# Layer norm statistics by bn_stats on transposed tiles, and twelve weight tiles whose low part is made by ScalarE and an adding DMA

## The chip, the core and the metric

The program runs on one core of a Trainium2 chip. The metric is the device time of one execution in microseconds (us). Five engines take part: PE (TensorE, matmuls and transposes), DVE (VectorE), ACT (ScalarE), POOL (GpSimd) and SP (SyncE, which issues the transfers). Each engine works through its own instructions in the order in which they were written.

## What is computed

One step of a backbone of four layers over 640 tokens (128 context tokens, 512 latent tokens) with 1024 features. The mixers are differential attention (layer 0 and again layer 3), retention (layer 1) and a short gated convolution (layer 2). What matters here is the end of each layer, the normalization, and the start of the next:

```
def layer_norm(x, g, b):
    xf = x.astype(jnp.float32)
    mu = jnp.mean(xf, -1, keepdims=True)
    var = jnp.mean(jnp.square(xf - mu), -1, keepdims=True)
    return ((xf - mu) * lax.rsqrt(var + LN_EPS)).astype(x.dtype) * g + b
...
hs = xs * (1 + sc_s) + sh_s            # modulated input of a layer's projection
...
xs = layer_norm(ALPHA * xs + g_s * out_s, ln_g[i], ln_b[i])
```

`out_s` is the mixer's output times its output projection. The next layer's projection needs the normalized and modulated row, so it cannot start on a token before that token's mean and variance are known.

## The kernel before

**Layout.** The running x lies in SBUF feature-major: `xT[128, 8, 640]`, eight blocks m of 128 features, all tokens along the free axis. Every large product is made of three fp32r matmuls from a high and a low part of each operand: `hH`, `hL` for the modulated input, `yh`, `yl` for the mixer's output, and `wh`, `wl` for a weight tile. A weight tile arrives by DMA in `raw`; ACT copies it to `wh` (rounded to fp32r), and DVE (at times POOL) writes `wl = raw - wh` (`convert`). Four tiles of layers 1 to 3 do not go through the ring of `wh`/`wl` but into spare space (`RA`, `FB`). In the text "y,W matmuls" are those of the output projection, "h,W matmuls" those of the next layer's projection.

**A layer's end.** The tokens are worked in two halves, hf0 and hf1 (256 and 384 tokens; in layer 3 384 and 256). The output projection's last group runs over the eight m of hf0 and then the eight m of hf1; each result is added to `xT` by one or two DVE instructions (`xT<-ps,mod,xT`). Then class `LN` normalizes that half.

**Layer norm before.** Ahead of the last group an estimate of the mean is taken off x (`center`, `spread`, `sub_c`). As the m of a half arrive, ACT squares them (`FA<-xT`), and DVE or POOL add up x and the squares over m (`reduce`, rows `FA<-FA,xT` and `FA<-FA`). When both sums are there, PE sums over the 128 partitions with one-column matmuls against `onesm` (`sums`), which puts one token on a partition; DVE makes the variance and the inverse root by Newton steps on two or three columns (`rsqrt`), spreads it over a diagonal (`FA<-ident,sm`), and PE broadcasts it to all partitions (`bcast`, `FA,pick`). The mean goes a shorter way (`shift`, ACT copies it to `FA`), and `sub_mean` takes it off x from SBUF (`xT<-xT,FA`, on DVE or POOL). `normal` multiplies by the broadcast root from PSUM (`xT<-xT,ps`). Per m there follow the affine step twice (ACT writes `hH`, ACT or DVE the same in full precision into `FA`, row `FA<-xT,Av,Bv`) and `hL = FA - hH`. Then the h,W matmuls of that m may run.

**Order.** No order is written by hand. `plan` keeps streams of items (the mixer's, the layer norm's, the weights', the modulation vectors' `mods_all`, whose matmuls are the rows `mraw,cpad`) and takes, at each step, the item that a small model of the engines (`Clock`, with `LAT` for the delay from one engine to another) expects to start soonest. An item marked `now` is taken as soon as it can be. `xtt` and `affine` choose between two engines by the same model; `BIAS_T` is what the affine step's ACT version may be later than DVE's and still be taken. So a change of one item's engines shifts the order near it.

Of the kernel before, what the change touches and what calls it, by code (L numbers as in the profile page):

```python
# [13 lines left out]
I32 = mybir.dt.int32  # L14
# [33 lines left out]
BIAS_T = 0.0  # L48
# [16 lines left out]
N_W = 0  # L65
C_OP = 0
# [13 lines left out]
GATE_L = 2000.0  # L80
GATE_H = [4000.0, 4000.0]
# [3 lines left out]
class W:  # L85


    def __init__(self, src, n=1024, direct=False, own=None, after=()):
        self.src, self.n, self.direct = src, n, direct
        self.own, self.after = own, after  # L90
        self.raw = self.hi = self.lo = self.slot = None
        self.uses = 0
# [19 lines left out]
class Clock:  # L112
# [4 lines left out]
    ENG = ("PE", "ACT", "DVE", "POOL", "DMA")  # L117
    LAT = {
        "PE": (0.0, 280.0, 250.0, 250.0, 2000.0),
        "ACT": (197.0, 34.0, 128.0, 80.0, 2000.0),  # L120
        "DVE": (196.0, 145.0, 127.0, 74.0, 2000.0),
        "POOL": (197.0, 170.0, 155.0, 102.0, 2000.0),
        "DMA": (1400.0, 1400.0, 1400.0, 1400.0, 2000.0),
# [19 lines left out]
    def arr(self, d, name, n):  # L143
        a = d.get(name)
        if a is None or a.shape[1] < n:
            b = np.full((5, max(n, 400)), -1e4)
# [15 lines left out]
    def run(self, ops, commit, gate=4000.0, slack=250.0):  # L162
# [9 lines left out]
        for eng, dur, outs, ins, port in ops:  # L172
# [11 lines left out]
            for oi, oo, e, end in own:  # L184
                if e == row == 4:
                    continue
# [38 lines left out]
def kernel(ctx: ExitStack, tc: tile.TileContext, io: dict):  # L225
# [21 lines left out]
    onesm = sb("onesm", [128, 128])  # L247
# [21 lines left out]
    onesr = sb("onesr", [128, 1], F32R)  # L269
# [150 lines left out]

    def copymax(out, a, mx):
# [10 lines left out]
    def dma(out, in_):  # L432
# [5 lines left out]
        do("DMA", n * 4 / 360.0, [out] if sb_o else [], [in_] if sb_i else [], lambda: nc.sync.dma_start(out=out, in_=in_))  # L438

# [168 lines left out]
    def outproj_items(l, wname, gi, groups, final=False, ln=None, need=()):  # L608
# [37 lines left out]
        for i, (mp, mi, hf) in enumerate(order):  # L646
# [10 lines left out]
            if final:  # L657
                late = [("y", base + grp[-1], h) for h in range(2)] + [("c", l, hf, 2 * mp + mi) if l == 1 else ("c", l, 1, 7)]
# [9 lines left out]
    class LN:  # L668

        def __init__(self, l, hf):
            self.l, self.hf = l, hf
            self.c0, self.n = HALF_F[l][hf]
            n = self.n
            o = NF - 7 * T if hf == 0 else NF - 7 * n
            v = [FA[:, o + i * n:o + i * n + n] for i in range(7)]
            self.dg = v[0]
            o = 0 if hf == 0 else T - n
            self.sc = KD[:, o:o + n] if l == 1 else RA[:, 4096 + o:4096 + o + n]  # L680
            self.db = v[1]
            buf = {0: FA[:, 4864:], 1: None, 2: F2[:, 6432:], 3: FA[:, 4864:]}[l]
            self.cs = None if buf is None else buf[:, o:o + n]
            self.sd, self.q = v[2:4]
            self.sq = self.t = v[4:7]
# [4 lines left out]
        def center(self):  # L690
            xtt(self.sc, self.x(0), self.x(1), ALU.add, BIAS_L)

        def spread(self):
            ps = pj((self, 0))[:, 0:self.n]
            mm(ps, onesr.to_broadcast([128, 128]), self.sc, True, True)

            if self.cs is not None:
                act(self.cs, ps)
                done((self, 0))

        def sub_c(self, m):
            x = self.x(m)
            if self.cs is not None:
                xtt(x, x, self.cs, ALU.subtract, BIAS_C)
                return
            vtt(x, x, bank((self, 0))[:, 0:self.n], ALU.subtract)
            if m == 7:
                done((self, 0))

        def add_q(self, m):  # L710
            if m:
                xtt(self.q, self.q, self.sq[m % 3], ALU.add, BIAS_L)

        def reduce(self, m):
            x = self.x(m)
            act(self.sq[m % 3] if m else self.q, x, ACTF.Square)
            if m:
                xtt(self.sd, self.x(0) if m == 1 else self.sd, x, ALU.add, BIAS_L)
                self.add_q(m - 1)
            if m == 7:  # L720
                self.add_q(7)

        def sums(self, which, src):
            ps = bank((self, 1)) if which else pj((self, 1))
            for i in range(self.n // 128):
                o = 8 * which + 2 * i
                mm(ps[:, o:o + 1], src[:, 128 * i:128 * i + 128], onesm[:, 0:1], True, True)

        def shift(self):
            ps = pj((self, 0))[:, 0:self.n]  # L730
# [3 lines left out]
            done((self, 0))  # L734
# [69 lines left out]
        def items(self):  # L804
            l, hf = self.l, self.hf
            it = []
            for m in range(8):
                it.append(Item(lambda m=m: self.reduce(m), need=[("x", l, hf, m)]))
            it.append(Item(self.mean))
            it.append(Item(self.var))  # L810
            it.append(Item(self.shift, give=[("db", l, hf)]))
            it.append(Item(self.bcast, give=[("rb", l, hf)]))
            ap, lo, sm_ = [], [], []
            for m in range(8):
                sm_.append(Item(lambda m=m: self.sub_mean(m), need=[("db", l, hf)], give=[("ctr", l, hf, m)]))
                nd = [("rb", l, hf), ("ctr", l, hf, m)]
                if l + 1 < DEPTH:
                    ap.append(Item(lambda m=m: self.apply_t(m), need=nd + [("aff", l + 1)] + ([("lnh", l, hf, m - 3)] if m > 2 else []),
                                   give=[("t", l, hf, m)]))
                    lo.append(Item(lambda m=m: self.apply_lo(m), need=[("t", l, hf, m)], give=[("lnh", l, hf, m)]))  # L820
                else:
                    ap.append(Item(lambda m=m: self.output(m), need=nd))
            return it, ap, lo, sm_

        def c_items(self, need):
# [1014 lines left out]
```

## Time and profile before

| | us |
|---|---|
| runs | 1867.8, 1868.26, 1870.71 |
| median of the runs | 1868.26 |
| the profiled execution, its own time | 1870.52 |
| its span from first to last instruction | 1868.6 |
| mean granted TensorE clock in it | 0.974 of full speed |
| PE busy | 1785.9 (96%) |
| DVE busy | 1200.9 (64%) |
| ACT busy | 731.2 (39%) |
| POOL busy | 195.8 (10%) |

The times are those of whole executions; the span is what the trace covers, 1.9 us less. Busy shares are averages over the span. Between the layers they look otherwise: the stretch of a layer boundary runs here from the first y,W matmul of the last group to the h,W matmul with which the next layer's first groups of weight tiles are through on both halves. There are three, at about 433 to 506, 1057 to 1141 and 1383 to 1465 us, and a tail from 1822 us in which layer 3 is normalized and written out.

### The profile page before, as it was taken

To read this page: it belongs to the slowest core of one execution; us is meant where nothing else is said; L and a number is where in the kernel's file an instruction comes from. 1 tells how busy PE (TensorE), PEld (TensorE's weight loads), DVE (VectorE), ACT (ScalarE), POOL (GpSimd) and SP (SyncE) were. 2 spreads that over 40 slices of the span, in tenths; PEclk is the share of its full clock that TensorE was granted. 3 is DMA by queue.
4 is the path that set the end of the run, shared out by engine and by line. 5 is a ranking of instruction groups with operands and counts; after the bars stand their busy time and mean duration, and the time that the engine had idled before them with its cause. 6 is when DMAs were issued, how large, how long until landed. Compare 5 with 4: busy or idle time off the path is not lost.

```text
span 1868.6 us, 34003 instructions
## 1 busy us (share of the span) xinstructions
PE 1785.9 (96%) x13644; PEld 1713.8 (92%) x13644; DVE 1200.9 (64%) x2854; ACT 731.2 (39%) x1607; POOL 195.8 (10%) x191
## 2 busy tenths in 40 slices
PE   7999999998999999999999989999998999999994
PEld 6999999997899989989998979999997999999994
DVE  3887778768936334345344686334478877877778
ACT  3555445533434333332222233222233455555532
POOL 2100000013300000000000113000311310000032
PEclk9999999998999999999999989999997999999997
DMA  9534332214213123223331341243333222312211
GB/s 339 159 111 125 111 111 86 77 49 147 78 46 100 68 90 125 84 75 124 104 100 46 102 136 46 85 136 119 102 103 115 70 65 66 90 56 71 63 32 57
DMA packets 74590, 180.64 MB, mean 97 GB/s; under 512 B 9408, under 2 KB 20800, under 8 KB 73408
## 3 DMA queue, kind: packets, MB, share of 16 engines
q1 hardware_dynamic: 74432, 178.47, 30.0%
q8 instruction: 107, 1.75, 0.4%
q14 instruction: 51, 0.42, 0.1%
HBM read 159.04 MB, written 8.91 MB: 90 GB/s over the span
## 4 chain that ended last, share of the span: by engine, by line
PE 78%; DVE 13%; ACT 5%; issue 2%; DMA 2%; SPq 0%; POOL 0%; DVEq 0%; ACTq 0%
PE ps L450 75%; PE ps L458 3%; DVE wl L377 2%; ACT FA L374 2%; DVE sm L408 2%; ACT wh L374 1%; DVE F L377 1%; DMA mraw<-in_w_mod 1%; DVE xT L377 1%; DVE RA L377 1%; DVE FA L425 1%; DVE FA L377 1%; ACT F L374 1%; DVE FA L408 1%; DVE F L430 1%
## 5 line engine op out<-in xcount | busy, mean ns | idle before, releaser
L450 PE MATMUL ps<-hH,wh 128*128 128x256 f32 (+1 forms) x1184 | 374.4, 316 | 6.0 <-ACT wh L374 3.1
L450 PE MATMUL ps<-wh,hH 128*128 128x256 f32 x1280 | 371.3, 290 | 1.6 <-DVE sm L425 0.9
L450 PE MATMUL ps<-hH,wl 128*128 128x256 f32 (+1 forms) x1184 | 368.1, 311 | 1.5 <-DVE wl L377 1.5
L450 PE MATMUL ps<-hL,wh 128*128 128x256 f32 (+1 forms) x1184 | 368.1, 311 | 0.2 <-DVE hL L377 0.2
L450 PE MATMUL ps<-wl,hH 128*128 128x256 f32 x1280 | 362.9, 284 | 0.0
L450 PE MATMUL ps<-wh,hL 128*128 128x256 f32 x1280 | 362.9, 284 | 0.0
L377 DVE TENSOR_TENSOR wl<-raw,wh 128x1024 fp32r<-128x1024 f32 (+2 forms) x183 | 217.6, 1191 | 147.0 <-ACT wh L374 139.3
L374 ACT ACTIVATE wh<-raw 128x1024 fp32r<-128x1024 f32 (+2 forms) x198 | 197.8, 1002 | 182.4 <-PE ps L450 144.1
L450 PEld LDWEIGHTS ps<-wh,hH 128*128 128x128 f32 x1280 | 246.3, 192 | 6.7 <-DVE sm L425 2.5
L450 PEld LDWEIGHTS ps<-wh,hL 128*128 128x128 f32 x1280 | 246.2, 192 | 0.6
L450 PEld LDWEIGHTS ps<-wl,hH 128*128 128x128 f32 x1280 | 245.9, 192 | 0.0
L450 PEld LDWEIGHTS ps<-hH,wh 128*128 128x128 f32 x1184 | 226.5, 191 | 11.7 <-issue 4.0
L450 PEld LDWEIGHTS ps<-hH,wl 128*128 128x128 f32 x1184 | 226.7, 191 | 2.1 <-DVE wl L377 2.1
L450 PEld LDWEIGHTS ps<-hL,wh 128*128 128x128 f32 x1184 | 226.3, 191 | 0.7 <-DVE hL L377 0.7
L450 PE MATMUL ps<-yh,wh 128*128 128x384 f32 (+1 forms) x640 | 201.1, 314 | 2.0 <-ACT yh L374 0.8
L450 PE MATMUL ps<-yl,wh 128*128 128x384 f32 (+1 forms) x640 | 198.4, 310 | 3.0 <-DVE yl L377 2.2
L450 PE MATMUL ps<-yh,wl 128*128 128x384 f32 (+1 forms) x640 | 198.1, 309 | 1.8 <-DVE wl L377 1.8
L374 ACT ACTIVATE FA<-FA,sm 128x640 f32<-128x640 f32 x144 | 111.9, 778 | 164.8 <-DVE sm L425 163.2
L408 DVE SCALAR_TENSOR_TENSOR xT<-ps,mod,xT 128x128 f32<-128x128 f32 (+2 forms) x312 | 121.3, 434 | 78.8 <-PE ps L450 76.5
L374 ACT ACTIVATE F<-ps 128x128 f32<-128x128 f32 (+2 forms) x338 | 98.3, 319 | 162.8 <-PE ps L450 160.0
L450 PE MATMUL ps<-RA 128*128 128x320 f32 (+2 forms) x696 | 129.8, 320 | 2.8 <-DVE F L408 1.8
L374 ACT ACTIVATE FA<-ps 128x512 f32<-128x512 f32 (+3 forms) x145 | 67.5, 470 | 161.8 <-PE ps L450 91.0
(171 smaller groups left out, 2792.7 us busy)
## 6 DMA issues: line engine op xcount, KB each, us to landing
mraw<-in_w_mod SPq DMA_DIRECT2D x160, 256.0 KB, 4.1
raw<-in_wqk_a SPq DMA_DIRECT2D x32, 512.0 KB, 3.6
raw<-in_wvz_a SPq DMA_DIRECT2D x32, 512.0 KB, 3.7
raw<-in_wvg_b SPq DMA_DIRECT2D x32, 512.0 KB, 3.5
raw<-in_win_c SPq DMA_DIRECT2D x32, 512.0 KB, 3.5
RA<-RA SPq DMA_DIRECT2D x32, 320.0 KB, 4.0
raw<-in_wqk_b SPq DMA_DIRECT2D x16, 512.0 KB, 3.5
raw<-in_wout_b SPq DMA_DIRECT2D x16, 512.0 KB, 3.5
```

Source lines behind the costliest of these rows:

```text
L374: do("ACT", d, outs, [in_] + extra, lambda: nc.scalar.activation(out=out, in_=in_, func=func, **k))
L377: do("DVE", n_of(out) / 0.96 + 70, [out], [a, b], lambda: nc.vector.tensor_tensor(out=out, in0=a, in1=b, op=op), both(a, b))
L408: lambda: nc.vector.scalar_tensor_tensor(out=out, in0=a, scalar=s, in1=b, op0=op0, op1=op1), both(a, b))
L425: do("DVE", n_of(out) / 0.96 + 68, [out, mx], [a], lambda: nc.vector.tensor_tensor_reduce(out=out, in0=a, in1=z, scale=-0.125, scalar=3.0e ...
L430: do("DVE", n_of(out) / 0.96 + 70, [out], [a], lambda: nc.vector.stream_shuffle(out=out, in_=a, mask=m))
L450: lambda: nc.tensor.matmul(out, lhsT=lhsT, rhs=rhs, start=start, stop=stop, skip_group_check=True))
L458: do("PE", 116.0, [out], [a], lambda: nc.tensor.transpose(out, a, ident))
```

## The change

1. `LN` takes its statistics in another way. PE transposes x, 128 tokens by four blocks m at a time, into one PSUM bank (`stats`, `tr`); DVE's `bn_stats` reads the 512 columns and writes six statistics for each token, `bn_aggr` joins the two halves of the features into mean and variance (`mean`). The mean is spread over a diagonal too and broadcast by matmuls (`shift`), and `sub_mean` reads it from PSUM on DVE. Its eight instructions are put between the Newton steps of the inverse root (`rsqrt`, `between`). `center`, `spread` of the estimate, `sub_c`, `reduce`, `add_q` and `sums` go, with `onesm` and `onesr`.
2. `mean` and `var` are `now` items in both halves, and the y,W matmuls of the last group no longer need the centered x.
3. The first four weight tiles (`N_ADD`) that a layer's first h,W matmuls use, in layers 1 to 3, get their low part in two steps: a second ACT pass writes `-raw` rounded to fp32r, and a DMA issued by GpSimd adds `raw` to it. `Clock` gets a sixth queue, `ADD`, for it.
4. `BIAS_T` goes from 0 to 1000: the affine step takes ACT wherever the model expects it up to 1 us later than DVE.

```diff
-BIAS_T = 0.0
+BIAS_T = 1000.0
...
+N_ADD = 4
...
+NOW = (0, 1)
...
+    def bstats(out, a):
+        do("DVE", n_of(a) / 0.96 + 70, [out], [a], lambda: nc.vector.bn_stats(out=out, in_=a), both(a, a))
+    def baggr(out, a):
+        do("DVE", 150.0, [out], [a], lambda: nc.vector.bn_aggr(out=out, in_=a.rearrange("p (c s) -> p c s", s=6)))
...
+    def add(out, in_):
+        do("POOL", 1000.0, [], [], lambda: None)
+        do("ADD", n_of(out) * 512 / 200.0, [out], [in_], lambda: nc.gpsimd.dma_start(out=out, in_=in_, accum_op=ALU.add))
...
-    def rsqrt(y, x, n):
-        t = small(n)
-        vts(y.bitcast(I32), x.bitcast(I32), -0.5, float(0x5F3759DF), ALU.mult, ALU.add)
-        for _ in range(3):
+    def rsqrt(y, x, n, steps=(-1, 0, 1, 2), t=None, between=()):
+        t = small(n) if t is None else t
+        gaps = iter(between)
+        def gap():
+            for fn in gaps:
+                return fn()
+        for i in steps:
+            if i < 0:
+                vts(y.bitcast(I32), x.bitcast(I32), -0.5, float(0x5F3759DF), ALU.mult, ALU.add)
+                continue
             vtt(t, x, y, ALU.mult)
+            gap()
             stt(t, t, -0.5, y, ALU.mult, ALU.mult)
+            gap()
             stt(y, t, 1.5, y, ALU.add, ALU.mult)
+            gap()
+        for fn in gaps:
+            fn()
+        return t
...
-                late = [("y", base + grp[-1], h) for h in range(2)] + [("c", l, hf, 2 * mp + mi) if l == 1 else ("c", l, 1, 7)]
+                late = [("y", base + grp[-1], h) for h in range(2)]
...
+            self.dg, self.db, self.dm = v[0:3]
+            self.t = v[3:6]
...
+        def stats(self, i, q):
+            if i == q == 0:
+                self.st, self.mv = small(12 * self.nt), small(2 * self.nt)
+            ps = pj((self, "s", i, q))
+            c = self.c0 + 128 * i
+            for m in range(4):
+                tr(ps[:, 128 * m:128 * m + 128], xT[:, 4 * q + m, c:c + 128])
+            st = self.st[:, 12 * i + 6 * q:12 * i + 6 * q + 6]
+            def rest():
+                bstats(st, ps)
+                done((self, "s", i, q))
+            defer(rest)
+        def spread(self, dg, v):
+            shape = [128, self.nt, 128]
+            vtt(dg.rearrange("p (i t) -> p i t", t=128), ident.unsqueeze(1).to_broadcast(shape),
+                v.unsqueeze(2).to_broadcast(shape), ALU.mult)
+        def mean(self):
+            for i in range(self.nt):
+                baggr(self.mv[:, 2 * i:2 * i + 2], self.st[:, 12 * i:12 * i + 12])
+            self.spread(self.dm, self.mv[:, 0::2])
+            nt = self.nt
+            self.v, self.r = small(nt), small(nt)
+            vts(self.v, self.mv[:, 1::2], LN_EPS, op0=ALU.add)
+            self.w = rsqrt(self.r, self.v, nt, (-1, 0))
+        def var(self):
+            rsqrt(self.r, self.v, self.nt, (1, 2), self.w, [lambda m=m: self.sub_mean(m) for m in range(8)])
+            done((self, 0))
+            self.spread(self.dg, self.r)
         def shift(self):
-            ps = pj((self, 0))[:, 0:self.n]
+            ps = pj((self, 0))
             for i in range(0, self.n, 128):
-                mm(ps[:, i:i + 128], onesm, self.sd[:, i:i + 128], i == 0, True)
-            act(self.db, ps)
-            done((self, 0))
-        def mean(self):
-            self.sums(0, self.sd)
-            nt = self.n // 128
-            self.v, r = small(nt), small(nt)
-            vcopy(r, bank((self, 1))[:, 0:2 * nt:2])
-            stt(self.v, r, -1.0, r, ALU.mult, ALU.mult)
-        def var(self):
-            nt = self.n // 128
-            self.sums(1, self.q)
-            ps = bank((self, 1))
-            v, r = self.v, small(nt)
-            stt(v, ps[:, 8:8 + 2 * nt:2], LN_EPS, v, ALU.add, ALU.add)
-            done((self, 1))
-            rsqrt(r, v, nt)
-            shape = [128, nt, 128]
-            vtt(self.dg.rearrange("p (i t) -> p i t", t=128), ident.unsqueeze(1).to_broadcast(shape),
-                r.unsqueeze(2).to_broadcast(shape), ALU.mult)
+                mm(ps[:, i:i + 128], ones, self.dm[:, i:i + 128], i == 0, True)
...
-            xtt(x, x, self.db, ALU.subtract, BIAS_O if self.l + 1 == DEPTH and self.hf == 0 else BIAS_M)
+            vtt(x, x, bank((self, 0))[:, 0:self.n], ALU.subtract)
...
+            for q in range(2):
+                for i in range(self.nt):
+                    it.append(Item(lambda i=i, q=q: self.stats(i, q), need=[("x", l, hf, m) for m in range(4 * q, 4 * q + 4)]))
+            it.append(Item(self.mean))
+            it[-1].after = True
+            it[-1].now = hf in NOW
+            it.append(Item(self.shift))
+            it.append(Item(self.var))
+            it[-1].now = hf in NOW
+            it.append(Item(self.bcast, give=[("rb", l, hf)]))
...
+    seen = {}
+    for it in main:
+        for w in it.ws:
+            key = [k for k in it.need if k[0] == "lnh"][:1]
+            if key and key[0][1] >= 0 and not w.direct:
+                ws = seen.setdefault(key[0][1], [])
+                if w not in ws and len(ws) < N_ADD:
+                    ws.append(w)
+                    w.early = True
...
+        if w.early:
+            act(lo, r, ACTF.Copy, scale=-1.0)
+            add(f32(lo), r)
+            return
         xtt(lo, r, f32(h), ALU.subtract, BIAS_W if w in first else None)
```

What moves is read from the two programs' instructions in their order on an engine, at the boundary of layers 1 and 2, the second of the three. First PE, from the end of the last group's y,W matmuls on hf1 to the first h,W matmuls: `mraw,cpad` are modulation matmuls of the next layer, of which the last four rows of eight are shown, `onesm,FA` the one-column sums of hf1, `hH,RA` and `hL,RA` the first h,W matmuls of hf0. Before:

```order
L450 MATMUL ps<-mraw_69,cpad 32x128 x4
L450 MATMUL ps<-mraw_70,cpad 32x128 x4
L450 MATMUL ps<-mraw_71,cpad 32x128 x4
L450 MATMUL ps<-mraw_72,cpad 32x128 x4
L450 MATMUL ps<-onesm,FA 128x1 x3
L450 MATMUL ps<-hH,RA 128x256 x2
L450 MATMUL ps<-hL,RA 128x256
```

After, at the same place:

```order
L464 MATMUL ps<-yh_84,wh_74 128x384
L464 MATMUL ps<-yh_84,wl_78 128x384
L464 MATMUL ps<-yl_89,wh_74 128x384
L472 MATMUL ps<-ident,xT 128x128 x12
L464 MATMUL ps<-hH,RA 128x256 x2
L464 MATMUL ps<-hL,RA 128x256
```

The 32 modulation matmuls that stood there have moved behind the first h,W matmuls, and twelve transposes of hf1's blocks m 4 to 7 stand ahead of these.

Second DVE, at hf1's statistics. `sm` are small columns, `FA<-ident,sm` the spread over the diagonal, `wl_80` and `wl_78` low parts of weight tiles, and `xT<-xT,ps` 128x384 in the changed program is a `sub_mean`. Before, the Newton steps go on behind the last row, eight more small instructions and the spread:

```order
L419 COPY sm<-ps 128x3
L408 SCALAR_TENSOR_TENSOR sm<-sm 128x3
L377 TENSOR_TENSOR wl_80<-raw_66,wh_76 128x1024
L377 TENSOR_TENSOR wl_78<-raw_67,wh_74 128x1024
L408 SCALAR_TENSOR_TENSOR sm<-ps,sm 128x3
L404 TENSOR_SCALAR sm<-sm 128x3
L377 TENSOR_TENSOR sm<-sm 128x3
L408 SCALAR_TENSOR_TENSOR sm<-sm 128x3 x2
```

After:

```order
L425 BN_STATS sm<-ps 128x6 x3
L428 BN_AGGR sm<-sm 128x2 x3
L380 TENSOR_TENSOR FA<-ident,sm 128x384
L407 TENSOR_SCALAR sm<-sm 128x3 x2
L380 TENSOR_TENSOR sm<-sm 128x3
L411 SCALAR_TENSOR_TENSOR sm<-sm 128x3 x2
L380 TENSOR_TENSOR wl_80<-raw_66,wh_76 128x1024
L380 TENSOR_TENSOR wl_78<-raw_67,wh_74 128x1024
L380 TENSOR_TENSOR sm<-sm 128x3
L380 TENSOR_TENSOR xT<-xT,ps 128x384
```

Three `bn_stats`, three `bn_aggr` and a second spread have come in, the `sub_mean` of hf1 stand between the Newton steps, and the two weight tiles have moved behind the first of these.

Third POOL, from the last weight tile that it converts in layer 1 to the end of the boundary, of the changed program alone; before, sums, `sub_mean` and two `hL` stood there.

```order
L383 TENSOR_TENSOR wl_78<-raw_67,wh_74 128x1024
L383 TENSOR_TENSOR RA<-FA,FB 128x512 x3
L452 DMA RA<-raw_68 128x1024
L452 DMA RA<-raw_66 128x1024
L452 DMA wl_77<-raw_67 128x1024
L452 DMA wl_79<-raw_68 128x1024
L383 TENSOR_TENSOR hL<-FA,hH 128x256 x6
L383 TENSOR_TENSOR hL<-FA,hH 128x384 x2
```

The four adding DMAs are issued together, ahead of all `hL` of the boundary, eight of which are now POOL's.

## Rows read from the trace of the kernel before

**Rows 1.** Windows of the three boundaries, the tail, and a clean stretch of layer 1.

```profile
core 0: us, PE busy (x) PEld busy (x) DVE busy (x) ACT busy (x) POOL busy (x), PEclk, DMA share, GB/s
432.90:506.50 73.60, 61.83 (x459) 57.10 (x459) 67.08 (x167) 30.57 (x62) 23.70 (x25) 0.86 0.36 115
1057.50:1140.70 83.20, 72.02 (x515) 66.00 (x514) 70.50 (x178) 29.98 (x60) 23.14 (x28) 0.88 0.32 102
1383.50:1465.30 81.80, 76.16 (x581) 71.00 (x580) 65.95 (x159) 32.05 (x65) 17.96 (x21) 0.87 0.29 97
1822.10:1868.60 46.50, 22.40 (x138) 21.34 (x136) 40.08 (x116) 13.12 (x26) 9.54 (x8) 0.70 0.16 57
507.00:1057.00 550.00, 545.76 (x3973) 517.83 (x3972) 251.19 (x473) 169.25 (x318) 8.08 (x6) 1.00 0.27 88
```

**Rows 2.** Timeline of PE, layers 1 to 2: start, us, instruction [idle before, releaser].

```profile
1057.55 0.36 PE L450 MATMUL ps<-yh,wh 128*128 128x256 f32 x1
...
1075.01 0.28 PE L450 MATMUL ps<-yh,wl 128*128 128x256 f32 x1
1075.13 0.28 PE L450 MATMUL ps<-yl,wh 128*128 128x256 f32 x1
...
1093.88 0.34 PE L450 MATMUL ps<-yl,wh 128*128 128x384 f32 x1
...
1101.41 0.77 PE L450 MATMUL ps<-hH,RA 128*128 128x256 f32 x2
...
1115.43 0.80 PE L450 MATMUL ps<-hH,RA 128*128 128x256 f32 x2
...
1122.64 0.28 PE L450 MATMUL ps<-hL,wh 128*128 128x256 f32 x1
...
1140.36 0.33 PE L450 MATMUL ps<-hH,wl 128*128 128x384 f32 x1
1140.53 0.33 PE L450 MATMUL ps<-hL,wh 128*128 128x384 f32 x1
```

**Rows 3.** Timeline of DVE, layers 1 to 2, around the first normal of hf0.

```profile
1089.05 0.36 DVE L408 SCALAR_TENSOR_TENSOR sm<-sm 128x2 f32<-128x2 f32 x2
1089.45 0.42 DVE L377 TENSOR_TENSOR FA<-ident,sm 128x256 f32<-128x256 f32 x1
...
1091.19 1.67 DVE L408 SCALAR_TENSOR_TENSOR xT<-ps,mod,xT 128x384 f32<-128x384 f32 x3
1092.77 0.41 DVE L377 TENSOR_TENSOR xT<-xT,ps 128x256 f32<-128x256 f32 x1
1093.22 0.60 DVE L404 TENSOR_SCALAR FA<-xT,Av,Bv 128x128 f32<-128x128 f32 x2
```

**Rows 4.** Groups by line and form, DVE: count | busy us, mean ns.

```profile
L377 DVE TENSOR_TENSOR wl<-raw,wh 128x1024 fp32r<-128x1024 f32 x158 | 195.5, 1239 | 128.0 <-ACT wh L374 120.4 <-PE ps L458 5.2 <-PE ps L450 1.6
L425 DVE CUSTOM_DVE_ANT_1 FA<-ps,zero 128x640 f32<-128x640 f32 x128 | 101.5, 821 | 28.1 <-PE ps L450 27.1 <-ACT F L374 0.8
L419 DVE COPY FA<-ps 128x512 f32<-128x512 f32 x32 | 22.0, 686 | 13.1 <-PE ps L458 12.7
```

**Rows 5.** Timeline of PE, transposes of layer 1.

```profile
1056.38 0.71 PE L458 MATMUL ps<-ident,FA 128*128 128x128 f32 x5
```

**Rows 6.** Timeline of PE, layers 2 to 3.

```profile
1421.78 0.56 PE L450 MATMUL ps<-hH,RA 128*128 128x256 f32 x1
...
1447.55 0.28 PE L450 MATMUL ps<-wl,hH 128*128 128x256 f32 x1
...
1465.17 0.28 PE L450 MATMUL ps<-wl,hH 128*128 128x256 f32 x1
```

**Rows 7.** Timeline of PE, layers 0 to 1.

```profile
506.40 0.34 PE L450 MATMUL ps<-hL,wh 128*128 128x384 f32 x1
```

**Rows 8.** Timeline of DVE, its last instruction.

```profile
1865.39 0.41 DVE L404 TENSOR_SCALAR xT<-xT,lng,lnb 128x256 f32<-128x256 f32 x1
```

**Rows 9.** From issue to landing of the weight tiles (tile raw).

```profile
DMA to landing us min/median/max: 2.5/3.5/13.8
```

More of the change, by code (lines that the diff above doesn't have):

```diff
@@ L80 @@
 GATE_L = 2000.0
+NOW = (0, 1)
+NOWA = ()
 GATE_H = [4000.0, 4000.0]
@@ L115 @@
     BLK = 32
-    ENG = ("PE", "ACT", "DVE", "POOL", "DMA")
+    ENG = ("PE", "ACT", "DVE", "POOL", "DMA", "ADD")
     LAT = {
[L119 to L123, printed above, removed]
+        "PE": (0.0, 280.0, 250.0, 250.0, 2000.0, 300.0),
+        "ACT": (197.0, 34.0, 128.0, 80.0, 2000.0, 1100.0),
+        "DVE": (196.0, 145.0, 127.0, 74.0, 2000.0, 1100.0),
+        "POOL": (197.0, 170.0, 155.0, 102.0, 2000.0, 0.0),
+        "DMA": (1400.0, 1400.0, 1400.0, 1400.0, 2000.0, 2000.0),
+        "ADD": (2000.0, 2000.0, 2000.0, 2000.0, 2000.0, 0.0),
     }
@@ L145, in arr @@
         if a is None or a.shape[1] < n:
-            b = np.full((5, max(n, 400)), -1e4)
+            b = np.full((6, max(n, 400)), -1e4)
             if a is not None:
@@ L184, in run @@
             for oi, oo, e, end in own:
-                if e == row == 4:
+                if e == row >= 4:
                     continue
@@ L674, in __init__ @@
             self.c0, self.n = HALF_F[l][hf]
+            self.nt = self.n // 128
             n = self.n
[L676 to L683, printed above, removed]
@@ L684, in __init__ @@
-            self.sd, self.q = v[2:4]
-            self.sq = self.t = v[4:7]
+            o = NF - 6 * T if hf == 0 else NF - 6 * n
+            v = [FA[:, o + i * n:o + i * n + n] for i in range(6)]
+            self.dg, self.db, self.dm = v[0:3]
+            self.t = v[3:6]
         def x(self, m):
             return xT[:, m, self.c0:self.c0 + self.n]
-        def center(self):
-            xtt(self.sc, self.x(0), self.x(1), ALU.add, BIAS_L)
-        def spread(self):
-            ps = pj((self, 0))[:, 0:self.n]
-            mm(ps, onesr.to_broadcast([128, 128]), self.sc, True, True)
-            if self.cs is not None:
-                act(self.cs, ps)
-                done((self, 0))
@@ L701, in sub_c @@
[L701 to L727, printed above, removed]
+        def stats(self, i, q):
[10 more added lines that the diff above has]
+            defer(rest)
@@ L806, in items @@
             it = []
-            for m in range(8):
[L808 to L816, printed above, removed]
+            for q in range(2):
[8 more added lines that the diff above has]
+            it.append(Item(self.bcast, give=[("rb", l, hf)]))
+            ap, lo = [], []
+            for m in range(8):
+                nd = [("rb", l, hf)]
                 if l + 1 < DEPTH:
@@ L819, in items @@
                                    give=[("t", l, hf, m)]))
+                    ap[-1].now = hf in NOWA
                     lo.append(Item(lambda m=m: self.apply_lo(m), need=[("t", l, hf, m)], give=[("lnh", l, hf, m)]))
@@ L822, in items @@
                     ap.append(Item(lambda m=m: self.output(m), need=nd))
-            return it, ap, lo, sm_
-        def c_items(self, need):
-            it = [Item(self.center, need=need), Item(self.spread)]
-            for m in range(8):
-                it.append(Item(lambda m=m: self.sub_c(m), give=[("c", self.l, self.hf, m)]))
-            for x in it:
-                x.limit = LIM_C
-            return it
+            return it, ap, lo
         def x_items(self):
@@ L1520 @@
         it.gate = 1e9
-    main, side_streams, ops_all, lx, mods_all, cc = [], [], [], [], [], []
-    lnst = [[[], [], [], []], [[], [], [], []]]
+    main, side_streams, ops_all, lx, mods_all = [], [], [], [], []
+    lnst = [[[], [], []], [[], [], []]]
     for l in range(DEPTH):
@@ L1544 @@
                     it.gate = GATE_L if d is not dst[0] else GATE_H[ln.hf] if n < 10 else GATE_L
-        before = [("op", 1, HB - 2), ("states", 1, HB - 1)] if l == 1 else [("op", l, C_OP)]
-        cc += lns[0].c_items(before) + lns[1].c_items(())
         lx += lns[0].x_items() + lns[1].x_items()
         ybase[0] += n_y[l]
-    streams = [ld0, st0, lo0, co] + lnst[0] + lnst[1] + side_streams + [mods_all, cc, x0, lx, main, ops_all]
+    streams = [ld0, st0, lo0, co] + lnst[0] + lnst[1] + side_streams + [mods_all, x0, lx, main, ops_all]
+    seen = {}
[7 more added lines that the diff above has]
+                    w.early = True
     for s in streams:
```

7 lines of the change are left out of this document (1 added, 6 removed).

## The prediction

> **What bounds the kernel now.** I first compared a clean stretch with the layer boundaries in the windows [rows 1]: from 507 to 1057 us PE is busy 545.8 of 550.0 us at full clock, so nothing but fewer matmuls would help there. At the three boundaries PE is busy 62 to 76 of 74 to 83 us although it works at a mean granted clock of only 0.86 to 0.88, while DVE is busy 67.1, 70.5 and 66.0 us: there DVE's chain through the layer norm sets the pace. A mean of 0.88 over 83.2 us means that a quarter of the stretch ran at the lower level (1.2 instead of 2.4 GHz), which cost some 10 us. In the tail the same chain ends the program.
>
> The timeline of PE shows the loss [rows 2]. At boundary 1 to 2 the last y,W matmul of hf0 is issued at 1075.13 and that of hf1 at 1093.88. The first h,W follow at 1101.41, but unbroken work starts only at 1115.43, and hf1's pass ends at 1140.53. From the starts of neighbours, a y,W or h,W matmul of 256 columns takes 0.12 us of PE and one of 384 takes 0.17. The stretch from 1057.55 holds 96 y,W and 72 h,W of either width, 168 x 0.12 + 168 x 0.17 = 48.7 us of the 83.0. With some 5 us of small matmuls, 29 us are loss. That is what a shorter layer norm can win.
>
> **The prices.** In the same stretch DVE's rows give [rows 3]: a Newton step 0.18 (two in 0.36), a spread 0.42, an x update of 384 columns 0.53 (three in 1.67), `normal` from PSUM 0.45 to the next start; a `sub_mean` from PSUM is the same form, 0.58 for 384 columns scaled by length. A weight tile's low part is 1.2 us [rows 4]. A transpose takes 0.11 us of PE (five in 0.71, the last one's length 0.28) [rows 5]. `bn_stats` is not in the trace. The nearest rows read PSUM as it does: the copy of 512 columns, 686 ns, and the custom reduction over 640 columns, 821 ns, which scales to 0.66 for 512 [rows 4]. I take 0.65 back to back, the copy's form being nearest. Below, it could hardly be under 0.55 (one column per step of the same two rows without their start); above, if it passed twice over the columns, 1.3. `bn_aggr` on 12 elements lies between a small step, 0.18, and 0.4; I take 0.2.
>
> **Boundary 1 to 2, walked along the changed order.** The start of the group stays. ACT gets two more passes of about 1 us for the spare tiles ahead of the next `yh`, and DVE loses the two low parts there; one stall for another, 0. Eight transposes in the y,W stream move hf0's last y,W from 1075.1 to 1076.0. Then the chain of hf0: last x update, eight transposes and the way to DVE 1.8; two `bn_stats` 1.3; two `bn_aggr` 0.4; spread 0.4; four small 0.8; an x update 0.5; eight `sub_mean` 3.6 and seven Newton steps 1.3, side by side in DVE's queue; spread 0.4; three x updates 1.6. That is 12.1 us, so the first `normal` starts at 1088.1 instead of 1092.8 [rows 3]. PE meanwhile runs hf1: 96 x 0.17 = 16.3 from 1076.0, with 24 transposes (2.6, and 2 of waiting for x updates and free banks) and picks, to 1099.7; the modulation matmuls, which before stood there and waited for their transfers, are behind. First h,W at 1099.7. The 72 of hf0 with 32 modulation matmuls in between reach hf1's `bcast` at 1109, where DVE is not ready: from 1099.8 three `bn_stats` 2.0, three `bn_aggr` 0.6, spread 0.5, small 0.8, the two weight tiles 2.4, eight `sub_mean` 4.7, Newton 1.3, spread 0.5 is 12.8, so 1112.6. PE waits 3.6 us there; what is queued behind the waiting pick are 18 h,W of hf0 that could run, and the pass of hf1. With them it ends at 1129.2 instead of 1140.5. I take 2.3 us off for work at the lower clock behind that wait: **-9**, between -4 (the wait on hf1 twice as long and the clock lost for as long as before) and -14 (no wait).
>
> **Boundary 2 to 3.** The h,W matmuls start at 1421.8 and the 96th is issued at 1447.55, 25.8 us for 96 x 0.12 = 11.5 of work [rows 6]. The same walk starts them at 1420.6 and needs 16.2, with a similar wait at hf1's `bcast`; the 120 behind take 18.8 against 17.6. End 1455.6 instead of 1465.2; less 1.1 for the clock, **-8.5** (-4 to -12).
>
> **Boundary 0 to 1.** DVE is full (67.1 of 73.6 us [rows 1]), and PE's stalls for x updates of hf1 (5.5 us in my walk) stay, since `bn_stats` and `sub_mean` now stand among them in DVE's queue. The walk ends at 499.9 against 506.4 [rows 7]; half of that I give to the lower clock behind those stalls: **-3.5** (0 to -6.5).
>
> **Tail.** DVE works without a break to 1865.8 [rows 8]. Sums leave it, ten `bn_stats` and all `sub_mean` of the last half from PSUM come; the difference in my count is **-2** (0 to -4).
>
> **Start and middle.** The order there is nearly the same; 0, give or take 1. All 160 transposes, 18 us, are inside the walks, as are the removed one-column sums. The affine steps that `BIAS_T` moves, 41 fewer on DVE at 0.3 us, lie on ACT, which is busy 30 of 83 us at a boundary [rows 1]; they are counted in the walks too.
>
> **The adding DMAs.** I cost them at nothing, since in my walk there are 12 us from the second ACT pass to the first use at boundary 1 to 2, and 7 at 0 to 1. No DMA issued by GpSimd is in the trace; the weight tiles on SP's queue land after 3.5 us in the middle and 13.8 at worst [rows 9]. From the one end nothing is paid, from the other each boundary loses up to 5 us. Queued behind the four issues on POOL are eight `hL`, for which PE would wait.
> The Trainium skill ("DMA: Bandwidth & Descriptors", section "Anatomy of one DMA — SWDGE (gpsimd) path") gives 2.0 us plus the bytes over 436e3 for such a transfer, 3.2 us for a tile of 512 KB; by that the adds would be in time, though the page fits plain transfers, and no run here shows one that adds.
>
> **Sum.** -9 - 8.5 - 3.5 - 2 = -23 us. The profiled execution took 1870.5 us itself, 2.3 above the median of the runs, 1868.3: 1847.5 for its like, **1845 us** on the median.
>
> **Rivals.**
> *The adds come late (0.20).* POOL issues four one after the other; if each takes 3 us or more, the fourth lands 12 us or later, which is past first use, the loads into the same `raw` buffers wait for it on SP's queue with the modulation weights behind, and the `hL` behind them are late as well. Against it, POOL is busy only 18 to 24 us at a boundary [rows 1]. It would give back 4 to 7 us at each of the three boundaries: 1857 to 1866, middle 1860.
> The Trainium skill has a rule that speaks for this one ("SBUF — State Buffer", section "Who interferes with whom"): GpSimd writes its descriptors through a port that it shares with DVE, and a DVE instruction in a two-port mode locks it out. By that the issues would wait for gaps in a DVE that is busy nine tenths of a boundary; the trace before has no GpSimd issue to show it.
>
> *`bn_stats` is slow (0.12), slower than before.* Ten stand at each boundary and ten in the tail, all on a DVE that sets the pace. Each 0.1 us above 0.65 costs 40 x 0.1 = 4 us, so the gain is gone at 1.2 us. At 1.3, a double pass, it is 26 us: 1871. Lower clock behind the longer waits would add to it, up to 1880. For it speaks only that no row shows the operation; against it, that the copy and the reduction from PSUM both run at a column a step.
>
> *The wait only moves (0.08).* PE gets 18 us of transposes, and these wait in its queue for x updates with h,W behind them, where modulation matmuls stood that needed no x. If those waits and the lower clock eat what DVE wins, the time stays within 0.2% (3.7 us, about what a measurement of this kernel can tell from no change): 1868. Against it: the lost 29 us at boundary 1 to 2 are more than the transposes there, 4.4 us.
>
> **Chances.** The forecast has 0.60, and its own range is 1834 to 1855, the bounds of the four terms not all taken at once. For the whole, up to 1866 takes in the late adds and part of the moved wait, and leaves out the slow `bn_stats` (0.12) and half of the no-change case; 1832 below leaves little: 1832 to 1866. Faster by over 0.2%: 0.60 and nearly all of the late adds, 0.79; within: 0.09; slower: 0.12.
>
> **What would show it.** Right: in the changed profile `bn_stats` near 0.65 us; the first `normal` of hf0 at boundary 1 to 2 some 30.5 us behind the group's first y,W matmul (35.2 before); first h,W at 42 us behind it and hf1's pass through at 74 (83.0 before); clock above 0.9 in that window; a wait of 3 to 4 us of PE at hf1's `bcast`. Wrong: PE waits for `RA` or `wl` released by a DMA of POOL's queue, or for `hL` on POOL (late adds); `bn_stats` over 1 us; waits of PE's transposes for `xT` of over 4 us in sum at a boundary; a stretch between boundaries that grew.

## The result, and the profile after

| | before | after |
|---|---|---|
| median of the runs, us | 1868.0 (4 runs, 1864.9 to 1870.7) | 1839.7 (4 runs, 1836.7 to 1841.6) |
| ratio to before, 95% interval | | 0.9848 [0.9827, 0.9868] |
| the profiled execution, its own time | 1870.5 | 1841.6 |
| its span | 1868.6 | 1839.9 |
| DVE busy | 1200.9 | 1138.6 |
| POOL busy | 195.8 | 127.4 |

The changed kernel is faster by 28.3 us, 1.5%; forecast were 23 us and 1845, with a range from 1832 to 1866. Between the two profiled executions lie 28.9 us.

The windows of the same four stretches and of the clean one, each from the first y,W matmul of a last group to the same count of h,W matmuls, answer to [rows 1]:

```profile
core 0: us, PE busy (x) PEld busy (x) DVE busy (x) ACT busy (x) POOL busy (x), PEclk, DMA share, GB/s
430.90:498.30 67.40, 60.12 (x478) 56.29 (x477) 54.49 (x140) 31.42 (x60) 23.56 (x28) 0.92 0.56 156
1052.10:1126.30 74.20, 68.06 (x533) 63.87 (x532) 51.59 (x139) 31.30 (x58) 21.66 (x28) 0.93 0.47 130
1368.80:1440.70 71.90, 69.72 (x594) 66.02 (x593) 51.89 (x133) 32.24 (x60) 22.12 (x28) 1.00 0.50 139
1797.90:1839.90 42.00, 25.04 (x160) 21.53 (x158) 33.07 (x96) 9.10 (x16) 4.55 (x5) 0.84 0.18 63
499.00:1050.00 551.00, 544.64 (x3963) 516.19 (x3962) 249.56 (x470) 168.62 (x316) 6.29 (x4) 1.00 0.28 88
```

DVE's work in a boundary falls from 66 to 70 us to 52 to 54 us, in a stretch that is 6 to 10 us shorter, and the granted clock rises from 0.86 to 0.88 to between 0.92 and 1.00. The clean stretch has the same clock, and PE's busy time in it differs by 1.1 us.

The timeline of PE at boundary 1 to 2 shows the steps [rows 2]:

```profile
1051.94 0.36 PE L464 MATMUL ps<-yh,wh 128*128 128x256 f32 x1
...
1056.95 0.58 PE L464 MATMUL ps<-yh,wh 128*128 128x256 f32 x1 [2.73 <-ACT yh L377]
...
1072.31 0.28 PE L464 MATMUL ps<-yl,wh 128*128 128x256 f32 x1
...
1092.67 0.34 PE L464 MATMUL ps<-yl,wh 128*128 128x384 f32 x1
...
1094.68 0.48 PE L464 MATMUL ps<-hH,RA 128*128 128x256 f32 x2
...
1104.91 0.93 PE L464 MATMUL ps<-FA,pick 128*128 128x128 f32 x6 [1.53 <-DVE FA L380]
...
1126.06 0.34 PE L464 MATMUL ps<-hL,wh 128*128 128x384 f32 x1
```

The h,W matmuls start 42.7 us behind the group's first y,W matmul (43.9 before) and from there run with one wait of 1.5 us for hf1's broadcast, where before 14 us passed between the first of them and unbroken work. hf1's pass ends 74.1 us behind the group's start, against 83.0. At the group's start, three stalls of 0.8, 0.8 and 1.3 us for `yl` and `yh` before have become two, of 0.8 us and of 2.7 for a `yh`. ACT's timeline has the cause of the longer one, four passes for the two spare tiles ahead of that `yh`:

```profile
1052.10 0.75 ACT L377 ACTIVATE yh<-ps 128x256 fp32r<-128x256 f32 x2
1052.73 3.89 ACT L377 ACTIVATE RA<-raw 128x1024 fp32r<-128x1024 f32 x4
1056.52 0.76 ACT L377 ACTIVATE yh<-ps 128x256 fp32r<-128x256 f32 x2
```

DVE's timeline of hf0 at the same boundary is the chain that the prediction walked [rows 3]:

```profile
1073.40 1.30 DVE L425 BATCH_NORM_STATS2 sm<-ps 128x6 f32<-128x512 f32 x2 [0.16 <-PE ps L472]
1074.62 0.33 DVE L428 BATCH_NORM_AGGREGATE sm<-sm 128x2 f32<-128x12 f32 x2
1074.98 0.42 DVE L380 TENSOR_TENSOR FA<-ident,sm 128x256 f32<-128x256 f32 x1
...
1076.72 0.15 DVE L380 TENSOR_TENSOR sm<-sm 128x2 f32<-128x2 f32 x1
1076.79 0.41 DVE L380 TENSOR_TENSOR xT<-xT,ps 128x256 f32<-128x256 f32 x1
1077.12 0.15 DVE L411 SCALAR_TENSOR_TENSOR sm<-sm 128x2 f32<-128x2 f32 x1
...
1078.79 1.08 DVE L380 TENSOR_TENSOR xT<-xT,ps 128x256 f32<-128x256 f32 x3
1079.79 0.42 DVE L380 TENSOR_TENSOR FA<-ident,sm 128x256 f32<-128x256 f32 x1
...
1082.78 0.62 DVE L411 SCALAR_TENSOR_TENSOR xT<-ps,mod,xT 128x384 f32<-128x384 f32 x1 [1.47 <-PE ps L464]
1083.32 0.41 DVE L380 TENSOR_TENSOR xT<-xT,ps 128x256 f32<-128x256 f32 x1
```

From the last y,W matmul of hf0, 1072.3, to the first `normal`, 1083.3, pass 11.0 us (17.6 before). The six Newton steps of `var` and the eight `sub_mean` take 3.1 us, from 1076.7 to 1079.8. The inverse root is ten instructions in both kernels. Now four stand in `mean` and six in `var`, not seven, and before, six and not eight followed the last row of the old DVE order. The root's spread is ready at 1080.2; then DVE waits 1.5 us for PE, whose broadcast of the root stands in its order at 1082.6, behind y,W matmuls of hf1.

The group of `bn_stats`, which the trace of before did not have (line 425, then 428):

```profile
L425 DVE BATCH_NORM_STATS2 sm<-ps 128x6 f32<-128x512 f32 x40 | 25.7, 687 | 1.6 <-PE ps L472 1.5
L428 DVE BATCH_NORM_AGGREGATE sm<-sm 128x2 f32<-128x12 f32 x20 | 2.6, 179 | 0.0
```

And the adding DMAs, by the list of DMA issues (KB each, us to landing) and by POOL's groups; the plain loads of the same size on SP's queue still land after 3.5 to 3.6 [rows 9]:

```profile
wl<-raw POOLq DMA_DIRECT2D x6, 512.0 KB, 4.9
RA<-raw POOLq DMA_DIRECT2D x4, 512.0 KB, 5.5
FB<-raw POOLq DMA_DIRECT2D x2, 512.0 KB, 6.1
```

```profile
L452 POOL DMA_DIRECT2D wl<-raw x6 | 5.2, 865 | 53.7 <-ACT wl L377 24.9 <-DVE xT L411 14.1 <-PE ps L464 8.2
L452 POOL DMA_DIRECT2D RA<-raw x4 | 3.5, 878 | 181.7 <-ACT RA L377 180.7 <-DMA raw<-in_win_c 1.0
L452 POOL DMA_DIRECT2D FB<-raw x2 | 1.9, 948 | 13.4 <-PE ps L464 12.6 <-PE ps L472 0.8
```

They cost POOL 0.9 us each. Loads on SP's queue wait for all twelve of them, but no wait of PE that the profile lists ends with one: the last `wl` add of the boundary is issued at 1085.3, and its tile's first matmul comes after 1096.

PE's waits for modulation weights, which lay at the three boundaries, are all but gone (us in total, times, longest; before, then after):

```profile
PE ps L450 <- DMA mraw<-in_w_mod: 12.5, 15, 2.2
PE ps L464 <- DMA mraw<-in_w_mod: 1.1, 1, 1.1
```

### The profile page after: what moved, and what is told of

Its sections match the earlier page's. It is cut to its first block, busy times and chain, and to the rows that moved or that the text cites. A ratio compares the mean times of both kernels' runs of the same rounds, so it can differ in the third digit from the quotient of the medians.

```text
span 1839.9 us, 33871 instructions
## 1 busy us (share of the span) xinstructions
PE 1775.7 (97%) x13716; PEld 1704.6 (93%) x13716; DVE 1138.6 (62%) x2732; ACT 730.2 (40%) x1589; POOL 127.4 (7%) x131
## 4 chain that ended last, share of the span: by engine, by line
PE 76%; DVE 15%; ACT 5%; issue 2%; DMA 1%; SPq 0%; ACTq 0%; DVEq 0%
PE ps L464 73%; PE ps L472 3%; DVE wl L380 2%; ACT FA L377 2%; DVE sm L411 2%; ACT wh L377 2%; DVE xT L380 1%; DVE F L380 1%; DVE FA L434 1%; DVE xT L411 1%; ACT F L377 1%; DVE FA L411 1%; DVE RA L380 1%; DVE F L411 1%; DVE sm L425 1%
## 5 line engine op out<-in xcount | busy, mean ns | idle before, releaser
L380 DVE TENSOR_TENSOR wl<-raw,wh 128x1024 fp32r<-128x1024 f32 (+2 forms) x177 | 207.0, 1171 | 152.9 <-ACT wh L377 145.8
L464 PEld LDWEIGHTS ps<-yh,wh 128*128 128x128 f32 x640 | 122.1, 191 | 10.6 <-ACT yh L377 3.7
```

What stands on the lines that cost most here:

```text
L380: do("DVE", n_of(out) / 0.96 + 70, [out], [a, b], lambda: nc.vector.tensor_tensor(out=out, in0=a, in1=b, op=op), both(a, b))
L464: lambda: nc.tensor.matmul(out, lhsT=lhsT, rhs=rhs, start=start, stop=stop, skip_group_check=True))
```

## The experiments

Theory A: the statistics' chain on DVE sets the boundaries, and the shorter chain brings the time. Theory B, the rival: what brings it is the relief of DVE from work that has nothing to do with the statistics (weights to ACT and DMA, affine steps to ACT). A third reading has no run of its own: the modulation matmuls have moved, and what brings the time is that PE no longer waits for their weights. Ratios are to the kernel before, run beside on the same chip.

"The four ends" are the three boundaries and the tail. The stretches outside them vary too: in the profiled executions without the 7 us wait of experiment 2, the first boundary starts between 429.6 and 433.5 us, and the clean stretch lasts 551 to 556. So a difference of 4 us between two totals need not come from the ends.

**1. The parts taken out one at a time.** Without the adds:

```diff
-N_ADD = 4
+N_ADD = 0
```

> The changed kernel without the adding DMAs (N_ADD 0): all low parts are made by DVE or POOL again. Theory A (the shorter statistics chain is what brings the time): of the four tiles at a boundary two have their low part made ahead of the chain, beside a PE stall of the same length, and two of 1.2 us each fall into the chain, so 3 x 2.4 = 7 us are lost: about 1847 us, between 1843 and 1850. Theory B (what brings the time is the relief of DVE from work that has nothing to do with the statistics): 12 x 1.2 = 14 us and more are lost, 1854 us or over. If the adds bring nothing, 1840.

With the affine step as before:

```diff
-BIAS_T = 1000.0
+BIAS_T = 0.0
```

> The changed kernel with BIAS_T 0: the affine step goes to ACT only where the model expects ACT to be sooner. Theory A: the 41 affine steps of 0.3 us, 12 us of DVE, lie mostly behind the first normal, where PE already has h,W matmuls to run; a third of them counts, 4 us: 1844. Theory B: all of them count, 1852. If ACT's longer queue delays hH as much as DVE gains, 1840 or less.

With both edits, that is, the layer norm alone:

> The layer norm part alone: N_ADD 0 and BIAS_T 0 in the changed kernel, so bn_stats, the now items and the moved modulation matmuls stay. Theory A: most of the 28 us is kept, 1850 (between 1846 and 1856). Theory B: it is nearly as slow as the kernel before, 1862 to 1868.

Measured: 1849.1 us, 0.9896 [0.9881, 0.9911] without the adds; 1847.2, 0.9886 [0.9868, 0.9904] with `BIAS_T` 0; 1851.1, 0.9910 [0.9896, 0.9925] with neither. So the layer norm alone brings 17 us of the 28, as A has it; what of that is `bn_stats`, `sub_mean` on DVE or the order of the items is not separated. The adds are worth 9 us with `BIAS_T` 1000, between A's 7 and B's 14, and 6 at the four ends alone. `BIAS_T` is worth some 7 with the adds, between A's 4 and B's 12 (its runs spread from 1844.0 to 1850.2), and 2 or 3 without them, which the intervals do not tell from nothing. Both together bring 12 us: each seems to bring more where the other is there.

**2. The same two in the kernel before.** The adds alone (the sixth queue of `Clock`, `add`, `seen` and the branch in `convert`, as in the change), then with `BIAS_T` 1000:

```diff
+N_ADD = 4
...
+        if w.early:
+            act(lo, r, ACTF.Copy, scale=-1.0)
+            add(f32(lo), r)
+            return
```

> The kernel before with the adding DMAs alone: the first four weight tiles of layers 1 to 3 get their low part by ACT and a DMA of GpSimd, the layer norm is the old one. If the adds bring the same without bn_stats as with it (there they were worth 9 us): 1859. If the old layer norm, whose sums and sub_mean also use POOL, is held up by the four issues of 0.9 us, or the old path does not end on the low parts: 1864 to 1870.

> The kernel before with the adding DMAs and BIAS_T 1000, all but the layer norm. With bn_stats both together were worth 11.6 us (1851.1 against 1839.7). Theory B, relief of DVE as such: the same 11 to 12 us here, 1857. Theory A, the old chain also waits for POOL, ACT and matmuls between its DVE steps, so relief is worth less: 1862 to 1868. Since the old layer norm has ACT square every block, more affine steps on ACT could make it slower than 1868.

Measured: 1874.1 us, 1.0040 [1.0025, 1.0055], and 1875.3, 1.0039 [1.0025, 1.0053]. The edits that are worth 12 us on top of the new layer norm cost 7 on top of the old one. So relief of DVE, as B has it, is not enough by itself. The trace of the adds alone shows two places where POOL holds the old layer norm up. One is in boundary 1 to 2; POOL and then DVE:

```profile
1089.01 0.88 POOL L446 DMA_DIRECT2D wl<-raw  x1 [4.25 <-ACT wl L377]
1089.58 3.78 POOL L383 TENSOR_TENSOR xT<-xT,FA 128x256 f32<-128x256 f32 x5
```

```profile
1084.22 0.42 DVE L380 TENSOR_TENSOR FA<-ident,sm 128x256 f32<-128x256 f32 x1
...
1090.68 0.42 DVE L380 TENSOR_TENSOR xT<-xT,ps 128x256 f32<-128x256 f32 x1 [3.48 <-POOL xT L383]
```

The root's spread is ready at 1084.6, but five `sub_mean` of hf0 stand on POOL behind the issue of the second `wl` add, which waits 4.25 us for ACT's pass, and the first `normal` waits 3.5 us for them. Even so this boundary lasts some 4 us less than before. The other place is ahead of its first y,W matmul: POOL holds back the old layer norm's `center` behind the issues for `RA`; the list of PE's waits (us in total, times, longest) has that as

```profile
PE ps L458 <- POOL KD L383: 7.0, 1, 7.0
```

The stretch between boundaries 0 to 1 and 1 to 2 is 8.6 us longer for it than before, and this is what makes the kernel slower.

The same trace speaks to the third reading. PE waits only 1.1 us for modulation weights in it, as after the change, but 19.6 us for `FA` from DVE (sums and spreads), where it waited 3.8 before. To lose the waits for modulation weights is thus not enough either; what share they have in the layer norm's 17 us is not shown.

**3. Is it POOL's queue?** The kernel before with `center` and `sub_mean` on DVE, without and with the adds:

```diff
-            xtt(self.sc, self.x(0), self.x(1), ALU.add, BIAS_L)
+            vtt(self.sc, self.x(0), self.x(1), ALU.add)
...
-            xtt(x, x, self.db, ALU.subtract, BIAS_O if self.l + 1 == DEPTH and self.hf == 0 else BIAS_M)
+            vtt(x, x, self.db, ALU.subtract)
```

> The kernel before with center and sub_mean on DVE alone, no adds: what the next run is compared with. Some 20 sub_mean at 0.35 to 0.47 us come to DVE from POOL, partly on the path: 1868 to 1876.

> The same with the adding DMAs. Theory P (in the old layer norm the adds hurt because center and sub_mean stand behind the issues in POOL's queue): with these two off POOL the 7 us loss is gone, and the adds bring time, 3 to 9 us against the run without them. Rival (the adds hurt by their transfers or by the lower clock, wherever POOL's other work is): 5 us or more slower than the run without them, as before.

Measured: 1872.4 us, 1.0026 [1.0015, 1.0037] without, and 1860.2, 0.9964 [0.9952, 0.9975] with the adds. With those two steps off POOL the adds bring 12 us, a little more than forecast, where they cost 7 before; 11 of them lie at boundary 1 to 2. So the relief that B means is worth as much with the old layer norm, once nothing that PE waits for stands behind the issues. The new layer norm, whose `sub_mean` read PSUM on DVE and which has no `center`, brings that about by itself: behind the issues on POOL there are only `hL`, which were not late. `center` and `sub_mean` were moved together, so no run parts them.

**4. What `bn_stats` may cost.** Each issued twice, in the same place:

```diff
-lambda: nc.vector.bn_stats(out=out, in_=a), both(a, a))
+lambda: (nc.vector.bn_stats(out=out, in_=a), nc.vector.bn_stats(out=out, in_=a))[1], both(a, a))
```

> The changed kernel with every bn_stats issued twice to the same columns, the order of all else unchanged: 40 more of 0.63 us, 25 us of DVE. The prediction priced each 0.1 us of bn_stats at 4 us, that is, all of it on the path: 1840 + 25 = 1865. Rival: only the last two or three of each half stand on the path, the first ones fill gaps in which DVE waits for PE: half or less of it, 1850 or under.

Measured: 1861.2 us, 0.9962 [0.9949, 0.9976], 21 us more for 40 further instructions, which at 0.61 us from start to start (not the 0.63 expected) are 24.5 us. Some 85% of what DVE gets to do here is paid (by the two intervals, between two thirds and all), near the prediction's price (3.5 us for each 0.1, not 4) and over the rival's half. The profiled execution has it where it should be: the four ends are 4.0, 5.5, 4.7 and 7.1 us longer, each with ten further instructions, 6.1 us.

**5. The place of the items.** `mean` and `var` not marked, and `sub_mean` behind the Newton steps:

```diff
-NOW = (0, 1)
+NOW = ()
```

> The changed kernel with mean and var not marked as now items: they wait for their turn in the model's order. If the place of these items carries a good part of the gain, 1846 to 1855; if the model would have chosen nearly the same place, 1840.

```diff
-            rsqrt(self.r, self.v, self.nt, (1, 2), self.w, [lambda m=m: self.sub_mean(m) for m in range(8)])
+            rsqrt(self.r, self.v, self.nt, (1, 2), self.w)
+            for m in range(8):
+                self.sub_mean(m)
```

> The changed kernel with the eight sub_mean behind the last Newton step instead of between the steps. In its trace seven Newton steps and eight sub_mean of 256 columns take 3.1 us interleaved, against the 4.9 us of the prediction's sum of their separate prices. If a Newton step that waits for the one before it costs its 0.2 us again when they stand apart: 1.3 to 1.8 us a half, all on the chain: three boundaries with two halves, the second partly hidden, and the tail: 1845 to 1851. If the two prices were simply too high: 1840.

Measured: 1845.3 us, 0.9885 [0.9870, 0.9899] for the first, between its two forecasts; boundary 2 to 3 alone is 4 us longer in it than after the change. The second took 1846.4, 0.9882 [0.9864, 0.9899]. In the second DVE shows the steps and the `sub_mean` apart:

```profile
1082.53 0.15 DVE L380 TENSOR_TENSOR sm<-sm 128x2 f32<-128x2 f32 x1
1082.72 0.36 DVE L411 SCALAR_TENSOR_TENSOR sm<-sm 128x2 f32<-128x2 f32 x2
...
1083.58 2.73 DVE L380 TENSOR_TENSOR xT<-xT,ps 128x256 f32<-128x256 f32 x8
1086.23 0.42 DVE L380 TENSOR_TENSOR FA<-ident,sm 128x256 f32<-128x256 f32 x1
```

From the first of the six steps to the spread 3.7 us pass, against 3.1 interleaved and 4.9 in the prediction, which counted seven. So both explanations hold in part: of the 1.8 us too many, 0.6 are the interleaving and 1.2 are prices and the step too many, above all 0.45 for a `sub_mean` that takes 0.33 when the next one is its like. That the whole time lies in the first forecast's range is luck. Of the 5.2 us between the two profiled executions only 1.4 lie at the four ends: boundary 0 to 1 is 2.3 us longer, 1 to 2 is 1.8 us shorter, 2 to 3 the same and the tail 0.9 longer. The rest lies where no `sub_mean` stands.

**6. Other tiles for the adds.** Two ring tiles a boundary and no spare ones:

```diff
-                    w.early = True
+                    w.early = not w.own
```

> The changed kernel with adding DMAs for the two ring tiles of each boundary only; the two spare tiles (RA, FB) get their low part from DVE again. PE waited 2.7 us for yh behind four ACT passes for RA at boundary 1 to 2 and lost some 3 us to the lower clock after it. If it is those passes that made that stall, and DVE has room ahead of the chain: 1837 to 1840. If the stall only moves back to yl, as in the kernel before: 1840 to 1842. If the two low parts of DVE fall into the chain: 1846.

Then, on top of that edit, four ring tiles:

```diff
-N_ADD = 4
+N_ADD = 6
```

> The changed kernel with adds for the first four ring tiles of a boundary and for none of the spare tiles: the two low parts of 1.2 us that stand in hf1's chain leave DVE too. If the chain sets hf1's time, 2 to 2.4 us a boundary against the variant with two ring tiles: 1833 to 1835. If the third and fourth issue, which now stand between the hL in POOL's queue and wait for ACT, hold up hL as sub_mean was held up in the old kernel: 1840 to 1850.

Measured: 1839.9 us, 0.9852 [0.9835, 0.9869], and 1841.6, 0.9869 [0.9849, 0.9888]. The first is the same as the change: with it boundary 1 to 2 lasts 72.3 us instead of 74.1, but the whole does not show it. The second lies in the range of its second forecast, but not by that mechanism: no wait of PE ends with an `hL` of POOL. DVE is rid of the two low parts and PE's wait for hf1's broadcast at boundary 1 to 2 falls from 1.5 to 0.6 us, but PE now waits for modulation weights, a load on SP's queue, nine times instead of once after the change:

```profile
PE ps L464 <- DMA mraw<-in_w_mod: 3.5, 9, 1.3
```

Around boundary 1 to 2, SP's queue waits four times for an adding DMA, against twice in the first variant, and the first of these loads is issued 53.6 us behind the group's start, against 49.6. That fits loads held up behind others that wait for the adds; no run parts it from the rest. No version clearly beats the changed kernel.

## Why the prediction held, point by point

**The mechanism** was the forecast one: DVE's chain set the boundaries, `bn_stats` cost 0.69 us (0.65 taken, 0.61 from start to start back to back), and PE had room for the 160 transposes. Experiment 4 shows that DVE paces the end of each layer, experiment 1 that the layer norm carries most of the gain. How much of that comes by the moved modulation matmuls stays open.

**Boundary 1 to 2**: -9 forecast, -8.9 measured (83.0 to 74.1). That it fits this well is luck, as errors cancel. hf0's last y,W came 20.4 us behind the group's start, not 18.5. "One stall for another, 0" for the ACT passes was 0.5 us short (stalls of 3.5 us, 3.0 before); the eight transposes took 1.6 us with their waits, not 0.9; and the rest, some 0.6 us, went to a longer stretch at the lower granted clock (6.8 us, 3.4 before). On the other side the chain behind it took 11.0 us, not 12.1: Newton steps and `sub_mean` 1.8 less, the way to DVE 0.7 less, the x updates 1.6 more, for most of which DVE waited for PE. So the first `normal` came 31.4 us behind the group's start, not 30.5, and the first h,W at 42.7, not 42. PE's wait for hf1's broadcast was 1.5 us, not 3.6, because Newton steps and `sub_mean` were priced too high there too.

**Boundary 2 to 3**: -8.5 forecast, -9.1 measured (81.6 to 72.5 us, from the same count of matmuls to the same). Here, too, errors cancel: the first h,W came 35.4 us behind the group's start, not 37.1, the 96 of hf0 took 15.0 us, not 16.2, and PE had no wait at hf1's broadcast, where a similar one was forecast; but the 120 behind took 22.1 us, not 18.8, with 96 modulation matmuls among them that stood further ahead before. Nothing was lost to the clock (granted 1.00), where 1.1 us were taken off. **Boundary 0 to 1**: -3.5 forecast, -5.9 measured (73.5 to 67.6 us), inside the bounds of that term. PE's transposes waited 3.9 us for x updates there, and half of the walk's 6.5 us had been given to the lower clock; the granted clock was 0.92 there, up from 0.86, so most of the walk's gain stayed. **Tail**: -2 forecast, -4.8 measured (from the same y,W matmul to the end 46.4 and 41.6 us), outside the term's bounds of 0 to -4, so this term was mis-sized: DVE's busy time there fell by 7 us, not by my count of 2, with twenty instructions fewer and `sub_mean` at 0.33 to 0.46 us.

**Start and middle**: 0 give or take 1 forecast. The first boundary starts 2.0 us earlier, and the stretch between the first and the second is 2.4 us longer. Before, the granted clock fell for 3.4 us at 291 us, after not, and 1.5 of the 2.0 us arise there; some of the experiments' kernels show this fall and some do not. Of the 2.4 us, 2.1 arise at one store of the state (`out_ns`), which landed 7.4 us after its issue, 5.2 before, with an ACT copy behind it. What sets either stays open; here the two cancel, but a stretch that grew was one of the prediction's signs of being wrong, and it grew. The sum of the six terms, -5.9 - 8.9 - 9.1 - 4.8 - 2.0 + 2.4, is -28.3, and 28.7 us lie between the spans; 0.3 lie between the second boundary and the tail.

**The rivals.** Late adds: they landed 4.6 to 6.9 us after issue, and no wait of PE ended with one, though loads on SP's queue waited for them. But the rival's other half, work held up behind the issues on POOL, is real: experiment 2 shows it with the old layer norm at 7 us of loss, and experiment 3 that it goes when that work is taken off POOL. The fit of the Trainium skill ("DMA: Bandwidth & Descriptors", section "Anatomy of one DMA — SWDGE (gpsimd) path"), by which 3.2 us was the estimate for a tile, was short for these adding transfers, which took 4.9 to 6.1 in the middle. The Trainium skill's rule on the shared port ("SBUF — State Buffer", section "Who interferes with whom") did not show: all twelve issues took 0.85 to 1.03 us with DVE busy 70 to 81% of the boundary. Whether DVE ran an instruction in a two-port mode beside them is not shown, so the rule is not refuted. Slow `bn_stats`: no, 0.69 us. The wait that only moves: PE's transposes waited 5.6 us for x updates in the whole execution, 11 times; 3.9 of it fell at boundary 0 to 1, just under the 4 us that were named as a sign.

**What was missed** is that the parts depend on each other. I costed the adds at nothing, which was right for their arrival. Their use was in the walks of the changed order but had no price of its own: taken out, they cost 9 us. That a step is hidden does not mean that it brings nothing; here it took two low parts off DVE's chain and two from ahead of it.

## What to carry to other kernels

Before work is moved to another engine's queue, look at what stands behind it there: the same adding DMAs cost 7 us where steps that PE or DVE waited for were queued behind their issues on POOL, and brought 9 to 12 us where only slack work was. Price each small instruction by the row in which it stands next to its like, and again by one where an independent instruction follows: a chain of dependent small steps has gaps that other work on the same engine fills in part (3.1 us against 3.7 here). When a chain on one engine sets a stage, doubling one of its instructions in place tells how much of what that engine does there is paid. And look at a changed time stage by stage before it is put down to an edit: a total in the forecast range can come from elsewhere.

## What the runs showed of the hardware

`bn_stats` over 512 columns in PSUM took 0.67 to 0.70 us, nearly what a copy of 512 columns took [rows 4], with 0.60 to 0.62 from one start to the next, and `bn_aggr` 0.18. A Newton step that waits for the one before it holds DVE for 0.2 us; with an independent `sub_mean` behind it the next instruction starts after 0.07 us. A DMA of GpSimd that adds one tile of 512 KB in SBUF to another took 0.9 us of POOL to issue and, by the middle of each kind of tile, 1.4 to 2.6 us longer to land than a plain load of the same size on SP's queue.
